# Layer 1 of a hybrid decoder step: queries, keys and values leave PSUM in one copy, and transposed keys leave their bank ahead of the queries

## The chip, the cores and the metric

The kernel runs on one core of a Trainium2 chip. The metric is the device time of one execution in microseconds (us). The engines are PE (TensorE), DVE (VectorE), ACT (ScalarE), POOL (GpSimd) and SP (SyncE, which issues the DMAs here).

## What is computed

The reference is one inference step of a two-layer decoder, for a prompt of 1024 tokens and 8 sample groups of 8 tokens (64 sample rows). Layer 0 is gated linear attention. Layer 1, which the change touches, is stick-breaking attention with 16 heads of 64:

```python
def sb_mixer(h, w_in, qn, kn, bias, w_out, k_past, v_past):
    ...
    u = h @ w_in
    q = rms_norm(u[..., :SB_W].reshape(bsz, length, SB_HEADS, SB_DH), qn)
    k = rms_norm(u[..., SB_W:2 * SB_W].reshape(bsz, length, SB_HEADS, SB_DH), kn)
    v = u[..., 2 * SB_W:3 * SB_W].reshape(bsz, length, SB_HEADS, SB_DH)
    g = u[..., 3 * SB_W:]
    ...
    o = sb_attend(q, k_all, v_all, bias, off).reshape(bsz, length, SB_W)
    return (o * jax.nn.silu(g)) @ w_out, k, v
```

In `sb_attend` the weight of key s for query t (s < t) is sigmoid(z[t, s]) times the product of (1 - sigmoid(z[t, j])) over the keys j between s and t. Normed keys and values are outputs too.

## The kernel before

Every fp32 operand of a large matmul is split into a high and a low half (`whi` and `wlo` for model weights, `qh` and `ql`, the halves of `kc`, the two `aT`), and products of halves are summed in PSUM. Layer 1 runs over 8 pairs of heads. For each pair, 9 tiles of rows (8 of 128 prompt rows, one of 64 sample rows) go through the input projection (`dense`, L293), and four times a gate's projection (`dense_t`, L315) stands between. Both sum in the two banks `acc`.

**Rows to queries and keys.** For each of the 9 tiles `qk_sums` squares queries and keys from the bank (ACT, L799), copies values (ACT, L801), sums the squares by head (DVE, L802) and takes the power -1/2 (POOL, L804). `qk_scale` multiplies queries and keys from the bank by it (DVE, L810) and makes the keys' output (POOL, L812). The bank is free after L810. The sample rows come out of `whole_rows` (L335, L336) in SBUF, as `xr`.

**Blocks.** Two tiles of rows at a time, 4 times a pair, `qk_p` transposes queries and keys on PE into one of the two banks `tr` (L829, four transposes). From there ACT copies the queries' high half four times (L853) and the keys' high half twice (L854, L855), and DVE makes the remainders: queries L856, L857, keys L858, L859. The text calls these the blocks 1 to 4 of a pair.

**Attention.** A unit is one head of the pair, 256 queries and 256 keys. `logits` multiplies (PE, L881, banks `z`) and ACT takes two sigmoids (`om` L884, `A` L885). `stick` scans on DVE (L904, L907) and multiplies (L912, L915). `turn` transposes the attention weights into a bank `tr` (PE, L928) and splits them (ACT L930, DVE L931). `weigh` multiplies by values (PE, L942, banks `o`). Behind a block's units `gate_b` adds two halves of the output (ACT L952, DVE L953, in turns) and multiplies by the gate (POOL, L954).

**What sets the order.** PE's order is written out: every step is put on one line of time by `at`, and PE follows it as it stands. Instructions of ACT, DVE, POOL and SP are put in order by the scheduler of the framework, by its own estimates. The scheduler also hands out the two buffers of each PSUM name; an instruction that writes a buffer waits for the last reader of what stood there. The next pair's model weights are split meanwhile (high halves ACT L219 or DVE L221, low halves POOL L222), most of it around block 4.

Of the kernel before, what the change touches and what calls it, by code (L numbers as in the profile page):

```python
# [9 lines left out]
F32 = mybir.dt.float32  # L10
# [3 lines left out]
AF = mybir.ActivationFunctionType  # L14
# [13 lines left out]
SH, DH = 16, 64  # L28
# [48 lines left out]
def tile_hybrid_decoder(ctx, tc, x_prompt, x_sample, state_gla, cache_k, cache_v, page_table,  # L77
# [3 lines left out]
    nc = tc.nc  # L81
# [46 lines left out]
    def sb(pool, name, shape, dtype=F32, bufs=2, tag=None):  # L128
        return pools[pool].tile(shape, dtype, name=name, tag=tag or name, bufs=bufs)
# [4 lines left out]
    def rows(t):  # L134
        return 128 if t < NP else NS
# [197 lines left out]
    def whole_rows(st, pool, n=512):  # L333
        up = sb(pool, "xr", [128, 512], F32, NX[pool])
        nc.scalar.activation(up[:64, :n], st["ps"][64:128, :n], AF.Copy)  # L335
        nc.vector.tensor_add(up[:64, :n], st["ps"][:64, :n], up[:64, :n])  # L336
        st["ps"] = up
# [78 lines left out]
    for t in range(NP + 1):  # L416
        st = {}
# [14 lines left out]
    for c, (c_0, n) in enumerate(CH):  # L432
        st = {}
# [228 lines left out]
    for h in range(GH):  # L662
# [3 lines left out]
        for c, (c_0, n) in enumerate(CH):  # L666
            st = {}
# [11 lines left out]
            for j, (key, out) in enumerate((("q", q_out), ("k", k_out))):  # L679
                lo, hi = a + (b - a) * 0.5 * j, a + (b - a) * 0.5 * (j + 1)  # L680
                dense_t(lo, hi, c_0, n, wqk,
                        lambda w, k, j=j: (w[k // 2], slice((k % 2) * 256 + j * 128, (k % 2) * 256 + j * 128 + 128)),
# [4 lines left out]
        for t in range(NP + 1):  # L687
            st = {}
# [50 lines left out]
    for c in range(2):  # L739
        w = weights([load_cols(w_out_a, D, k, c * 512, 0, 1, 512) for k in range(NK)])  # L740
        for t in range(NP + 1):
            st = {}
# [48 lines left out]
    def qk_sums(st, p, t):  # L791
        n = rows(t)
        if t == NP:
            whole_rows(st, "at1", 384)
        ps = st["ps"]
        sq = K1["sq"]
        q4 = ps[:n, :256].rearrange("p (h d) -> p h d", d=DH)
        ms = small.tile([128, 4], F32, name="ms4")
        nc.scalar.activation(sq[:n, :, :DH], q4, AF.Square, scale=1.0 / 8.0)  # L799
        st["v"] = sb("at1", "v", [128, 128])  # L800
        nc.scalar.activation(st["v"][:n], ps[:n, 256:384], AF.Copy)  # L801
        nc.vector.tensor_reduce(ms[:n], sq[:n], axis=AX.X, op=OP.add)  # L802
        st["rs"] = small.tile([128, 4], F32, name="rs4")
        nc.gpsimd.tensor_tensor(st["rs"][:n], ms[:n], half_exp[:n], op=OP.pow)  # L804

    def qk_scale(st, p, t):
        n, ps, rs = rows(t), st["ps"], st["rs"]
        q4 = ps[:n, :256].rearrange("p (h d) -> p h d", d=DH)
        qk = st["qk"] = sb("at1", "qk", [128, 4, DH], F32, 4)
        nc.vector.tensor_mul(qk[:n], q4, rs[:n, :, None].to_broadcast([n, 4, DH]))  # L810
        st["kout"] = sb("at1", "kout", [128, 2, DH])
        nc.gpsimd.tensor_mul(st["kout"][:n], qk[:n, 2:], K1["kn"][:n, None].to_broadcast([n, 2, DH]))  # L812

# [13 lines left out]
    def turn_qk(st, n, tr, slots):  # L827
        for j, x in enumerate(slots):
            nc.tensor.transpose(tr[:, x, :n], st["qk"][:n, 2 * j:2 * j + 2].rearrange("p a d -> p (a d)"), ident[:n, :n])  # L829
# [7 lines left out]
    def qk_p(sts, pair):  # L837

        tr = psum.tile([128, 4, 128], F32, name="tr")
        for x, st in enumerate(sts):
            turn_qk(st, 128, tr, (x, 2 + x))
        tr = tr.rearrange("p a s -> p (a s)")
        qp, kp, g = tr[:, :256], tr[:, 256:], K1["gains"]
        qh, kc = sb("at2", "qh", [128, 2, 256], F32R, NQ), sb("at2", "kc", [128, 2, 256], F32R, NKV)
        ql = K1["ql"][K1["turn"] % NQ]
        K1["turn"] += 1
        pair["q"].append((qh, ql))
        pair["k"].append(kc)  # L850
        up, dn = slice(0, 64), slice(64, 128)
        for dst, j, src in ((up, 0, up), (dn, 1, dn), (dn, 0, up), (up, 1, dn)):
            nc.scalar.activation(qh[dst, j], qp[src], AF.Copy, scale=g[src])  # L853
        nc.scalar.activation(kc[up, 0], kp[up], AF.Copy)  # L854
        nc.scalar.activation(kc[dn, 1], kp[dn], AF.Copy)  # L855
        nc.vector.scalar_tensor_tensor(ql[up, 0], qp[up], g[up], qh[up, 0], op0=OP.mult, op1=OP.subtract)  # L856
        nc.vector.scalar_tensor_tensor(ql[dn, 1], qp[dn], g[dn], qh[dn, 1], op0=OP.mult, op1=OP.subtract)  # L857
        nc.vector.tensor_sub(kc[dn, 0], kp[up], kc[up, 0])  # L858
        nc.vector.tensor_sub(kc[up, 1], kp[dn], kc[dn, 1])  # L859

    def gate_t(st, p, m, pair):
        ps, gt = st["ps"], sb("at1", "gt", [128, 256], F32, NG)
# [127 lines left out]
    for p in range(PAIRS):  # L990
# [4 lines left out]
        def columns(t, i, span):  # L995
            st = {}
            dense(i, t, w, st, span, 384)
            e = i + span
            at(e + 0.02, qk_sums, st, p, t)
            at(e + C_SC, qk_scale, st, p, t)  # L1000
            sts.append(st)
            if t < NP:
                at(max(e + C_SC, open2), v_parts, st, t, pair)
            if t == NP:
                at(e + C_TS, qk_s, st, p)
            elif t % 2 == 1:
                at(max(e + C_T, open2 + 0.01 * t), qk_p, sts[t - 1:], pair)
            at(max(e + C_T, open2) + 0.2, kv_store, st, p, t)
            return e
# [8 lines left out]
        for m in range(NP // 2):  # L1018
# [20 lines left out]
            if p == PAIRS - 1:  # L1039
                st = {}  # L1040
                for g in range(4):
                    n = 2 if g < 3 else 1
# [163 lines left out]
    for c, t in steps[:2 * NP - TAIL] + [(0, NP), (1, NP)] + steps[2 * NP - TAIL:]:  # L1206
        if t == NP and c == 0:
            i = max(i, s1 + S_GAP)
        st = {}
# [44 lines left out]
```

## Time and profile before

| | |
|---|---|
| Time, median of 3 runs | 1350.44 us (1347.35 to 1350.93) |
| The profiled execution | 1349.09 us, span 1347.4 us |
| PE busy over the span | 1269.9 us (94%) |
| DVE, ACT, POOL busy | 1011.1 (75%), 708.4 (53%), 515.5 (38%) us |
| TensorE clock granted | full in all 40 slices |
| DMA | 115.80 MB, mean 86 GB/s |

Busy times are sums over the instructions of an engine. A wait is the time an engine stood idle ahead of an instruction, put down to what was finished last among the things that it waited for. Layer 1's attention lies between about 535 and 1190 us of the span; a pair takes about 85 us there.

### The profile page before, as it was taken

To read this page: it belongs to the slowest core of one execution; us is meant where nothing else is said; L and a number is where in the kernel's file an instruction comes from. 1 tells how busy PE (TensorE), PEld (TensorE's weight loads), DVE (VectorE), ACT (ScalarE), POOL (GpSimd) and SP (SyncE) were. 2 spreads that over 40 slices of the span, in tenths; PEclk is the share of its full clock that TensorE was granted. 3 is DMA by queue.
4 is the path that set the end of the run, shared out by engine and by line. 5 is a ranking of instruction groups with operands and counts; after the bars stand their busy time and mean duration, and the time that the engine had idled before them with its cause. 6 is when DMAs were issued, how large, how long until landed. Compare 5 with 4: busy or idle time off the path is not lost.

```text
span 1347.4 us, 23358 instructions
## 1 busy us (share of the span) xinstructions
PE 1269.9 (94%) x8025; PEld 1128.5 (84%) x8025; DVE 1011.1 (75%) x2047; ACT 708.4 (53%) x1640; POOL 515.5 (38%) x847
## 2 busy tenths in 40 slices
PE   6899999999999999989989999899998999999998
PEld 5788888888887787889989899898898998978665
DVE  7857858759565357698898988988889889896543
ACT  6446245254352034566666766667667677763221
POOL 6222323223222215363453734646446464443000
PEclk9999999999999999999999999999999999999999
DMA  6311402403327443020120200202002022134862
GB/s 193 91 41 44 135 20 59 124 17 100 121 90 240 135 137 117 20 73 27 34 71 23 71 27 28 79 23 70 28 28 77 21 78 86 33 124 152 316 204 79
DMA packets 118456, 115.80 MB, mean 86 GB/s; under 512 B 11002, under 2 KB 97922, under 8 KB 118338
## 3 DMA queue, kind: packets, MB, share of 16 engines
q1 hardware_dynamic: 118338, 114.31, 27.5%
q8 instruction: 64, 1.05, 0.3%
q14 instruction: 54, 0.44, 0.1%
HBM read 83.61 MB, written 30.67 MB: 85 GB/s over the span
## 4 chain that ended last, share of the span: by engine, by line
PE 56%; DVE 25%; ACT 7%; issue 5%; POOL 4%; DMA 3%; SPq 0%; DVEq 0%; POOLq 0%; ACTq 0%
PE acc L293 33%; PE acc L315 6%; DVE run L907 4%; PE z L881 3%; PE tr L928 3%; PE o L942 2%; DVE aT L931 2%; DVE whi L221 2%; ACT qh L853 2%; DVE qk L810 1%; POOL rs L804 1%; DVE A L912 1%; DVE A L915 1%; PE o L544 1%; DVE run L904 1%
## 5 line engine op out<-in xcount | busy, mean ns | idle before, releaser
L293 PE MATMUL acc<-whi,h 128*128 128x512 f32 (+1 forms) x1728 | 538.1, 374 | 9.3 <-DVE qk L810 6.2
L293 PEld LDWEIGHTS acc<-whi,h 128*128 128x128 f32 x1728 | 312.8, 189 | 40.3 <-ACT sh L952 3.8
L293 PE MATMUL acc<-wlo,h 128*128 128x512 f32 (+1 forms) x864 | 322.6, 373 | 3.9 <-DVE wlo L222 2.5
L315 PE MATMUL acc<-h,whi 128*128 128x256 f32 (+5 forms) x832 | 191.7, 316 | 19.1 <-DVE qk L810 8.7
L222 POOL TENSOR_TENSOR wlo<-wr,whi 128x512 fp32r<-128x512 f32 x98 | 144.4, 1478 | 127.4 <-DVE whi L221 92.5
L293 PEld LDWEIGHTS acc<-wlo,h 128*128 128x128 f32 x864 | 162.5, 188 | 22.1 <-DVE wlo L222 3.2
L315 PEld LDWEIGHTS acc<-h,whi 128*128 128x128 f32 (+2 forms) x832 | 137.8, 185 | 26.2 <-issue 10.6
L907 DVE TENSOR_TENSOR_SCAN run<-om,run 128x256 f32<-128x256 f32 x192 | 141.8, 779 | 15.6 <-ACT om L884 15.1
L930 ACT ACTIVATE aT<-tr 128x512 fp32r<-128x512 f32 (+1 forms) x160 | 89.0, 556 | 82.8 <-PE tr L928 80.9
L884 ACT ACTIVATE om<-z,bias 128x512 f32<-128x512 f32 (+1 forms) x160 | 103.1, 644 | 48.3 <-PE z L881 39.6
L293 PE MATMUL acc<-w,h 128*128 128x384 f32 (+1 forms) x480 | 122.0, 365 | 0.8 <-DVE qk L810 0.8
L315 PE MATMUL acc<-h,wlo 128*128 128x256 f32 (+2 forms) x392 | 122.2, 312 | 0.3 <-POOL wlo L222 0.3
L931 DVE TENSOR_TENSOR aT<-tr,aT 128x512 fp32r<-128x512 f32 (+1 forms) x160 | 100.9, 631 | 9.7 <-ACT aT L930 7.4
L928 PE MATMUL tr<-ident,A 128*128 128x128 f32 x576 | 90.0, 274 | 18.6 <-DVE kc L859 8.4
L885 ACT ACTIVATE A<-z,bias 128x512 f32<-128x512 f32 (+1 forms) x160 | 102.4, 640 | 0.0
L942 PE MATMUL o<-aT,v 128*128 128x256 f32 (+1 forms) x640 | 98.1, 274 | 0.0
L928 PEld LDWEIGHTS tr<-ident,A 128*128 128x128 f32 x576 | 68.9, 140 | 34.0 <-ACT sq L799 9.0
L942 PEld LDWEIGHTS o<-aT,v 128*128 128x128 f32 x640 | 94.4, 188 | 1.7 <-DVE aT L931 1.0
L804 POOL TENSOR_TENSOR rs<-ms,half_exp 128x4 f32<-128x4 f32 (+1 forms) x72 | 86.2, 1198 | 21.3 <-DVE ms L802 18.8
L881 PE MATMUL z<-kc,qh 128*128 128x256 f32 x320 | 84.4, 286 | 7.2 <-DVE kc L858 7.2
L293 PEld LDWEIGHTS acc<-w,h 128*128 128x128 f32 x480 | 83.2, 189 | 6.3 <-issue 0.8
L899 POOL COPY run<-run 128x2 f32<-128x2 f32 x96 | 32.8, 342 | 135.7 <-DVE run L907 78.1
(273 smaller groups left out, 2488.7 us busy)
## 6 DMA issues: line engine op xcount, KB each, us to landing
wr<-in_w_in_b_dram SPq DMA_DIRECT2D x64, 256.0 KB, 3.0
wr<-in_w_in_a_dram SPq DMA_DIRECT2D x32, 256.0 KB, 2.9
kp<-in_cache_k_dram SPq DMA_DIRECT2D x16, 512.0 KB, 4.6
vp<-in_cache_v_dram SPq DMA_DIRECT2D x16, 512.0 KB, 4.9
o_d<-og SPq DMA_DIRECT2D x60, 128.0 KB, 1.8
x<-in_x_prompt_dram SPq DMA_DIRECT2D x8, 512.0 KB, 5.2
wr<-in_w_in_a_dram SPq DMA_DIRECT2D x32, 128.0 KB, 3.9
n<-in_state_gla_dram SPq DMA_DIRECT2D x8, 512.0 KB, 4.2
```

What stands on the lines that cost most here:

```text
L222: engine.tensor_sub(e.lo[:, :m], raw[:, :m], e.hi[:, :m])
L293: nc.tensor.matmul(st["ps"][:x.shape[1], :n], x, (w[k].hi if part == 0 else w[k].lo)[:, :n], start=first, stop=last)
L315: nc.tensor.matmul(st[key][:x.shape[1], :n], x, y, start=first, stop=last)
L804: nc.gpsimd.tensor_tensor(st["rs"][:n], ms[:n], half_exp[:n], op=OP.pow)
L881: nc.tensor.matmul(out, lhs, rhs, start=x == 0, stop=x == len(mm) - 1)
L884: nc.scalar.activation(u["om"][:, v0:], z[:, v0:], AF.Sigmoid, scale=-1.0, bias=K1["bias"][:, 1, hd:hd + 1])
L885: nc.scalar.activation(u["A"][:, v0:], z[:, v0:], AF.Sigmoid, bias=K1["bias"][:, 0, hd:hd + 1])
L907: nc.vector.tensor_tensor_scan(run[:, a, n - 1::-1], rev, rev, before[:, a, 0:1], op0=OP.mult, op1=OP.bypass)
L928: nc.tensor.transpose(tr[:, x], u["A"][:, col:col + 128], ident)
L930: nc.scalar.activation(hi[:, v0:], tr[:, v0:], AF.Copy)
L931: nc.vector.tensor_sub(lo[:, v0:], tr[:, v0:], hi[:, v0:])
L942: nc.tensor.matmul(q["po"][:, j, q0:], vs, part[:, x * 256 + q0:(x + 1) * 256], start=first and n == 0, stop=last and n == 3)
```

## The change

`qk_sums` makes one ACT copy of all 384 columns from the bank into a tile `qkv` in SBUF (four buffers); squares and products then read that tile, and the product is written in place. `qk_p` takes keys first, one engine after the other: ACT copies a high half, DVE takes its remainder, and so on for both halves of the keys and then of the queries. The two further query copies read the copies made before, in SBUF, and no longer the bank with a scale.

```diff
@@ qk_sums
-        q4 = ps[:n, :256].rearrange("p (h d) -> p h d", d=DH)
+
+        all3 = sb("at1", "qkv", [128, 384], F32, 4)
+        nc.scalar.activation(all3[:n], ps[:n, :384], AF.Copy)
+        st["qk"], st["v"] = all3[:, :256].rearrange("p (h d) -> p h d", d=DH), all3[:, 256:]
         ms = small.tile([128, 4], F32, name="ms4")
-        nc.scalar.activation(sq[:n, :, :DH], q4, AF.Square, scale=1.0 / 8.0)
-        st["v"] = sb("at1", "v", [128, 128])
-        nc.scalar.activation(st["v"][:n], ps[:n, 256:384], AF.Copy)
+        nc.scalar.activation(sq[:n, :, :DH], st["qk"][:n], AF.Square, scale=1.0 / 8.0)
@@ qk_scale
-        n, ps, rs = rows(t), st["ps"], st["rs"]
-        q4 = ps[:n, :256].rearrange("p (h d) -> p h d", d=DH)
-        qk = st["qk"] = sb("at1", "qk", [128, 4, DH], F32, 4)
-        nc.vector.tensor_mul(qk[:n], q4, rs[:n, :, None].to_broadcast([n, 4, DH]))
+        n, rs, qk = rows(t), st["rs"], st["qk"]
+        nc.vector.tensor_mul(qk[:n], qk[:n], rs[:n, :, None].to_broadcast([n, 4, DH]))
@@ qk_p
-        for dst, j, src in ((up, 0, up), (dn, 1, dn), (dn, 0, up), (up, 1, dn)):
-            nc.scalar.activation(qh[dst, j], qp[src], AF.Copy, scale=g[src])
         nc.scalar.activation(kc[up, 0], kp[up], AF.Copy)
+        nc.vector.tensor_sub(kc[dn, 0], kp[up], kc[up, 0])
         nc.scalar.activation(kc[dn, 1], kp[dn], AF.Copy)
+        nc.vector.tensor_sub(kc[up, 1], kp[dn], kc[dn, 1])
+        nc.scalar.activation(qh[up, 0], qp[up], AF.Copy, scale=g[up])
         nc.vector.scalar_tensor_tensor(ql[up, 0], qp[up], g[up], qh[up, 0], op0=OP.mult, op1=OP.subtract)
+        nc.scalar.activation(qh[dn, 1], qp[dn], AF.Copy, scale=g[dn])
         nc.vector.scalar_tensor_tensor(ql[dn, 1], qp[dn], g[dn], qh[dn, 1], op0=OP.mult, op1=OP.subtract)
-        nc.vector.tensor_sub(kc[dn, 0], kp[up], kc[up, 0])
-        nc.vector.tensor_sub(kc[up, 1], kp[dn], kc[dn, 1])
+
+        nc.scalar.activation(qh[dn, 0], qh[up, 0], AF.Copy)
+        nc.scalar.activation(qh[up, 1], qh[dn, 1], AF.Copy)
```

The new lines are L799 (copy), L802 (square), L803, L805, L809 (sums, power, product), L811 (keys' output), L851 to L854 (keys, ACT and DVE in turns), L855 to L858 (queries, likewise), L860 and L861 (copies in SBUF). Lines behind them stand 2 further down: the attention weights' copy L930 is now L932, their remainder L931 is L933, the scans L904 and L907 are L906 and L909. PE runs the same instructions in the same order; the order of the others is made anew.

DVE around block 4 of a pair, before. The scans are named SCALAR_TENSOR_TENSOR in the order and TENSOR_TENSOR_SCAN in the profile; `xr` are the sample rows.

```order
L912 TENSOR_TENSOR A<-A,run 128x256
L856 SCALAR_TENSOR_TENSOR ql_5790<-tr,gains,qh 64x256
L857 SCALAR_TENSOR_TENSOR ql_5790<-tr,gains,qh 64x256
L858 TENSOR_TENSOR kc<-tr,kc 64x256
L859 TENSOR_TENSOR kc<-tr,kc 64x256
L931 TENSOR_TENSOR aT_10136<-tr,aT_10135 128x512
L336 TENSOR_TENSOR xr<-acc,xr 64x384
L907 SCALAR_TENSOR_TENSOR run<-om,run 128x256 x2
L915 TENSOR_TENSOR A<-A,run 128x512
```

The same place with the change:

```order
L914 TENSOR_TENSOR A<-A,run 128x256
L852 TENSOR_TENSOR kc<-tr,kc 64x256
L854 TENSOR_TENSOR kc<-tr,kc 64x256
L933 TENSOR_TENSOR aT_10101<-tr,aT_10100 128x512
L336 TENSOR_TENSOR xr<-acc,xr 64x384
L856 SCALAR_TENSOR_TENSOR ql_5790<-tr,gains,qh 64x256
L909 SCALAR_TENSOR_TENSOR run<-om,run 128x256 x2
L917 TENSOR_TENSOR A<-A,run 128x512
L858 SCALAR_TENSOR_TENSOR ql_5790<-tr,gains,qh 64x256
L933 TENSOR_TENSOR aT_10160<-tr,aT_10159 128x384
```

The four operations of the block stood together; now attention weights, sample rows, two scans and a product stand between them.

ACT at the same place, with the change (before, L853 four times, L854 and L855 stood in one run, and `whi`, `aT`, `xr`, `om` and `A` followed):

```order
L851 ACTIVATE kc<-tr 64x256
L853 ACTIVATE kc<-tr 64x256
L932 ACTIVATE aT_10100<-tr 128x512
L219 ACTIVATE whi<-wr 128x512
L335 ACTIVATE xr<-acc 64x384
L855 ACTIVATE qh<-tr,gains 64x256
L886 ACTIVATE om<-z,bias 128x512
L887 ACTIVATE A<-z,bias 128x512
L219 ACTIVATE whi<-wr 128x512
L860 ACTIVATE qh<-qh 64x256
L799 ACTIVATE qkv<-xr 64x384
L219 ACTIVATE whi<-wr 128x512
```

L857, the second half of the queries, comes next; L853, L855 and L857 each wait for the DVE operation of the block ahead of them.

## Rows read from the trace of the kernel before

**Rows 1.** Windows: length; busy PE, PEld, DVE, ACT, POOL; PEclk; DMA share, GB/s.

```profile
535.00:1190.00 655.00, 610.82 (x4247) 582.97 (x4246) 564.53 (x1083) 445.70 (x952) 332.24 (x565) 1.00 0.17 49
784.00:869.20 85.20, 79.40 (x556) 75.77 (x555) 73.84 (x141) 57.41 (x122) 43.16 (x74) 1.00 0.16 45
840.00:860.00 20.00, 16.71 (x109) 15.09 (x107) 19.65 (x32) 14.89 (x32) 17.28 (x18) 1.00 0.35 100
```

**Rows 2.** Waits of PE, 530 to 1200: us in total, times, longest.

```profile
PE acc L315 <- DVE qk L810: 10.4, 7, 1.7
PE tr L928 <- DVE kc L859: 8.4, 6, 2.4
PE z L881 <- DVE kc L858: 7.2, 10, 1.4
PE acc L293 <- DVE qk L810: 7.0, 14, 1.2
PE tr L928 <- ACT sq L799: 4.5, 7, 1.0
```

**Rows 3.** Waits of DVE, the same stretch.

```profile
DVE ql L856 <- ACT kc L855: 34.2, 20, 4.8
```

**Rows 4.** Waits of ACT, the same stretch.

```profile
ACT sh L952 <- DVE og L953: 33.1, 20, 2.1
```

**Rows 5.** Instructions by form, 530 to 1200: busy us, mean ns.

```profile
L853 ACT ACTIVATE qh<-tr,gains 64x256 fp32r<-64x256 f32 x128 | 60.2, 470 | 21.6 <-PE tr L829 19.9
...
L930 ACT ACTIVATE aT<-tr 128x384 fp32r<-128x384 f32 x62 | 30.5, 491 | 43.7 <-PE tr L928 43.3
...
L799 ACT ACTIVATE sq<-acc 128x256 f32<-128x256 f32 x62 | 23.9, 385 | 11.6 <-DVE ms L802 6.6 <-PE acc L293 4.9
...
L801 ACT ACTIVATE v<-acc 128x128 f32<-128x128 f32 x62 | 17.6, 284 | 0.0
...
L859 DVE TENSOR_TENSOR kc<-tr,kc 64x256 fp32r<-64x256 f32 x32 | 13.6, 426 | 0.6
...
L855 ACT ACTIVATE kc<-tr 64x256 fp32r<-64x256 f32 x32 | 12.2, 380 | 0.6
...
L799 ACT ACTIVATE sq<-xr 64x256 f32<-64x256 f32 x8 | 3.3, 409 | 0.0
```

**Rows 6.** Line L810, whole span: ns min/median/max by form.

```profile
L810 DVE TENSOR_TENSOR qk<-acc,rs x64: 391/420/426, 527.6 to 1176.2; 128x256 f32<-128x256 f32 x64
...
L810 DVE TENSOR_TENSOR qk<-xr,rs x8: 406/1176/1514, 600.2 to 1194.8; 64x256 f32<-64x256 f32 x8
```

**Rows 7.** Timeline around block 4: start, us, instruction, idle before it.

```profile
845.36 0.47 DVE L856 SCALAR_TENSOR_TENSOR ql<-tr,gains,qh 64x256 fp32r<-64x256 f32 x1
...
846.11 0.69 ACT L884 ACTIVATE om<-z,bias 128x512 f32<-128x512 f32 x1
...
847.35 0.52 PE L928 MATMUL tr<-ident,A 128*128 128x128 f32 x3 [1.17 <-DVE kc L859]
...
849.82 1.51 DVE L915 TENSOR_TENSOR A<-A,run 128x512 f32<-128x512 f32 x1
...
851.38 0.66 PE L928 MATMUL tr<-ident,A 128*128 128x128 f32 x4
...
854.38 1.39 POOL L222 TENSOR_TENSOR wlo<-wr,whi 128x512 fp32r<-128x512 f32 x1
...
854.88 1.18 DVE L810 TENSOR_TENSOR qk<-xr,rs 64x256 f32<-64x256 f32 x1
```

**Rows 8.** Timeline at block 3 of the next pair.

```profile
909.31 0.69 DVE L915 TENSOR_TENSOR A<-A,run 128x512 f32<-128x512 f32 x1
...
910.75 0.38 ACT L855 ACTIVATE kc<-tr 64x256 fp32r<-64x256 f32 x1
...
911.17 0.48 DVE L856 SCALAR_TENSOR_TENSOR ql<-tr,gains,qh 64x256 fp32r<-64x256 f32 x1 [1.16 <-ACT kc L855]
...
912.73 0.35 PE L881 MATMUL z<-kc,qh 128*128 128x256 f32 x1 [0.54 <-DVE kc L858]
```

## What I expect of the change, and why

> **What bounds the kernel now.** The busy times by stretch come first [rows 1]. TensorE's granted clock is 1.00 throughout, so no clock is to be won back. In the 655.00 us of layer 1's attention part PE works 610.82, DVE 564.53, ACT 445.70, POOL 332.24. PE is the bound, and what the change can win on it is at most the 44 us in which PE idles. DVE stands close behind with 86%. The two further lines show where: one pair of heads lasts about 85 us, and in the 20 us from 840 to 860 DVE works 19.65. There the next pair's weights are split, DVE is the bound, and PE loses 3.3 us.
>
> The waits of PE say what ends its idle time [rows 2]. The two `acc` lines on the product L810 hold 10.4 + 7.0 = 17.4 us: a PSUM bank is not free before its rows have been squared, summed, raised to a power on POOL and multiplied. The `tr` and `z` lines belong to the blocks that turn queries and keys (`qk_p`). Waiting for L859 (8.4 us) is waiting for the bank of the block; for L858 (7.2 us) it is for finished keys. A transpose of weights needs nothing from the square L799: those 4.5 us are the same bank, whose last reader L859 ends just ahead of the square that the profile names. The waits of the other two engines show how such a block runs: DVE waits 34.2 us for ACT's last copy L855 before its first operation L856 [rows 3], and in `gate_b`, where the two engines take turns at one bank, ACT waits 33.1 us in 20 places for DVE [rows 4].
>
> **Part 1, the copy.** One ACT copy takes the place of the reading of PSUM by the square, the copy of values and the product. Its nearest row is a copy of the same form, 0.49 us (L930, 128x384); the values' copy of 0.28 us goes [rows 5]. That is 72 x 0.2 = 15 us more on ACT, which idles 209 us in the stretch: nothing on the path. The square reads SBUF now: for the sample rows, which were in SBUF already, it takes 0.41 instead of 0.39 us [rows 5], again nothing. PE's 17.4 us of waiting should go, since a copy that waits for the bank's matmuls alone ends about 0.5 us behind them and PE does not come back to the bank before the other one is filled: **-17.4**.
>
> The product is the price. From PSUM it took 0.39 to 0.43 us in all 64 places; from SBUF it took 1.18 us in the median of 8 [rows 6]; the one at 854.88 began beside POOL's L222, which reads SBUF, and ended 0.3 us behind it [rows 7]. All 72 read SBUF now. Lower bound nothing (0.41 us was also seen), upper bound 72 x 0.76 = 55 us of DVE time. What POOL does right behind the power decides: in the new order 49 of 72 times that is `kout`, which itself waits for the product, or a two-column copy; 23 times it is something longer. 23 x 0.76 = 17.5 us, and of a pair's nine products two fall into the stretch in which DVE is full, so that PE feels 2/9 of it: **+4**.
>
> The Trainium skill has this as a rule (SBUF — State Buffer, section "Who interferes with whom"): a VectorE instruction with two inputs in SBUF contends with a GpSimd instruction that reads SBUF, and the later one waits for the whole of the other; one with at most one input in SBUF does not. The trace agrees with both halves [rows 6]. Taken to its end, with every product behind a POOL operation, it makes the last rival below.
>
> **Part 2, the block.** Before, ACT ran six copies without a stop (4 x 0.47, 2 x 0.38) and DVE four operations behind them (two of about 0.43, two of about 0.47) [rows 5, 7]: 4.5 us to the release. Now ACT and DVE alternate: 0.38 + 0.43 + 0.38 + 0.43 + 4 x 0.47 = 3.5 us, and 7 handovers of 0.04 (L855 ends at 911.13, L856 begins at 911.17 [rows 8]): 3.8 us. Two copies of queries read SBUF; they have no scale, so I price them between L855's 0.38 and the old 0.47, on ACT beside other work: nothing. But that is an undisturbed chain. The orders of ACT and DVE show other work between its links, and each link waits for the other engine's queue. PE's order is unchanged, so the four blocks of a pair can be walked one by one.
>
> Block 1: the transposes that waited 7 times for the bank, 4.5 us, now get the other `tr` bank in the built kernel: **-4.5**. Block 2 had no stall and keeps slack. In the first pair the waits for keys (about 3 of the 7.2 us; seven third blocks hold the rest) should go, because ACT and DVE have little else to do there: **-3**.
>
> Block 3: DVE is free at 910.00 [rows 8]. From there, by when each ends: first subtraction 910.42, second key copy 910.84, second subtraction 911.3, ACT's copy of attention weights (0.49) 911.3, copy of q, k and v 911.8, first queries 912.3, their remainder 912.8, the square and the SBUF copy 913.05. PE had its keys at 912.73; it waits 0.3 longer, and up to 1.3 if it comes earlier by what it saved and DVE does not follow. I take 0.8 in each of 7 pairs: **+5.6**.
>
> Block 4 lies where DVE is full. DVE reaches the block at 845.36 [rows 7]. The second key copy waits for the subtraction that begins then; ACT, which ran through all its copies before, now ends the key copies at 846.2, the attention weights behind them at 846.8, a weight's high half and the sample rows at 847.9, the first queries at 848.4, and only then begins `om`, at 846.11 before. Behind it stand the second half of the queries and DVE's two scans and product (L907, L915), so the last reader of the bank, L858 in the new numbering, ends near 852.85. The first transposes after the block have the other bank, and wait for its reader as long as now for this one (1.17 us); the next ones, at 851.38 [rows 7], want the block's bank and wait about 1.4 us. With none of these delays the last reader ends at 850.3, and the old stall of 1.17 goes; with the longer form of L915 (1.51 us) it is some 0.8 later still. So -1.2 to +2.2 a pair, and I take +1.4 in 7 pairs, since ACT's order is certain: **+9.8**.
>
> One assumption in this walk is that a wait covers the whole bank. The trace shows it: L856 reads partitions 0 to 63 and still waits for L855, which reads 64 to 127 [rows 3].
>
> The Trainium skill would have it otherwise (PSUM — Partial Sum Buffer, section "PSUM bank collisions raise a hardware error"): two engines collide only on the same bank and the same 32 partitions, reads included, so the upper and lower halves need not wait for each other. By that, ACT would pass block 4 at its old time, its bank would be free by about 851, and blocks 3 and 4 would cost nothing: 5.6 + 9.8 = 15.4 us less than my sum, 1328. The waits in this program are by bank, so the sum goes by the row.
>
> **Sum**, against the profiled execution (1349.09 us, span 1347.4): 1349.1 - 17.4 + 4 - 4.5 - 3 + 5.6 + 9.8 = **1343.6**. That execution stands 1.35 us under the median of the runs, within their spread of 3.6. A difference under 0.3% (4 us) can't be told from none here.
>
> **Rivals.**
> *All waits go.* If the new order hides both blocks 3 and 4, PE gains the rest of its `tr` and `z` lines too: 17.4 + 8.4 + 7.2 + 4.5 = 37.5 us [rows 2], 1312. For it speaks that an undisturbed block is 0.7 us shorter and keys and first queries are ready 1.3 us sooner (2.7 against 4.0); against it that DVE is full around block 4 whatever the order is. A lesser form of it: if a wait covers only the half of the partitions that both engines read, both blocks cost nothing and the time is 1328; [rows 3] speaks against it, so 0.03. Chance 0.13 with that, anywhere from 1312 to 1335.
>
> *No change.* DVE is the bound wherever PE waits most: of the 3.3 us that PE loses from 840 to 860 [rows 1] nothing comes back if the same DVE work ends at the same time. If the longest stalls at the product (10.4 us) stay in this way, under another name, 1343.6 + 10.4 = 1354 is the far end, and half of it 1349. Chance 0.18.
>
> *The bank is held (slower).* Place: block 4, and the third block behind it. The taking of turns has a price in this program: ACT's wait in `gate_b` is 33.1 / 20 = 1.7 us a time [rows 4], and a block now has three such waits. If they delay the release not to 852.85 but two more turns, to 856, the transposes at 851.38 wait 4.7 us instead of 1.4, and `om` and the scans behind them move with it: 7 x 3.3 = 23, and 1343.6 + 23 = 1367. It decides as soon as blocks 3 and 4 cost more than the 17.4 + 4.5 + 3 - 4 = 20.9 us of the other terms, 3.0 us a pair; my sum has 2.2. Chance 0.18.
>
> *The product blocks DVE (slower).* If POOL is in the way of nearly all 72 products, DVE gains 55 us and works 95% of the stretch; with half of that on PE's path instead of 4 us, 1343.6 + 23 = 1367. Against it: after the power POOL mostly has nothing long to do. Chance 0.11.
>
> **Numbers.** My forecast, 1336 to 1346, has 0.40. Faster: 0.40 + 0.13 = 0.53; same 0.18; slower 0.18 + 0.11 = 0.29. The range leaves out the lower half of the first rival and the far end of the two slow ones, under 0.2 in all: 1318 to 1367.
>
> **What would show it.** Right: no PE wait for the product in the `acc` lines; no block-1 stall; in block 4 a wait of the weights' transposes for the last remainder of queries (L858) of 1 to 2 us a pair; ACT waits behind L853 for DVE; products of 0.42 us in some places and of over 1 us in others. Wrong: `acc` waits that stay because ACT's copy comes late; PE waits in blocks 3 and 4 above 3 us a pair or none; products that are all short or all long; DVE's busy time up by over 20 us.

## The result, and the profile after

The changed kernel takes 1360.92 us (median of 4 runs, 1358.62 to 1361.91) against 1349.93 us of the kernel before in the same comparison: a ratio of 1.0084, 95% interval 1.007 to 1.0097. It is slower by 11 us, where I had forecast that it would be faster by about 6. The profiled execution took 1361.91 us, with a span of 1360.1.

The waits of PE in the changed kernel, 530 to 1210 (us in total, times, longest), answer to [rows 2]:

```profile
PE tr L930 <- DVE aT L933: 19.6, 20, 2.5
PE z L883 <- ACT qh L860: 13.9, 10, 2.1
PE tr L828 <- DVE kTs L834: 5.3, 7, 1.3
PE tr L930 <- DVE ql L858: 5.2, 5, 1.0
PE tr L930 <- DVE A L914: 4.4, 6, 0.8
PE o L944 <- DVE aT L933: 4.2, 5, 0.9
```

No `acc` line is left: the 17.4 us of waiting for the product are gone, as the change promises. But the other lines have grown to over 50 us, and all of PE's waits together are more than before. PE now waits for a `tr` bank whose last reader is the remainder of the attention weights (L933), for the first queries in SBUF (L860), for the sample rows' keys (L834), for DVE's attention products (L914). All but L860 are DVE's.

ACT's longest line stands against [rows 4]; it is new:

```profile
ACT kc L853 <- DVE kc L852: 62.7, 32, 5.0
ACT sh L954 <- DVE og L955: 37.5, 19, 2.5
```

At the second key copy, L853, ACT stands 62.7 us, once in each of the 32 blocks, and behind it in ACT's queue stand copies that PE needs. ACT's wait in the turns of `gate_b` is little changed (37.5 us; before 33.1).

The windows of one pair, of the 20 us from its block 4 on, and of 5 us around a later wait answer to [rows 1] (length; busy PE, PEld, DVE, ACT, POOL; granted clock; DMA):

```profile
783.50:869.50 86.00, 78.76 (x555) 75.70 (x555) 75.17 (x141) 58.44 (x123) 44.06 (x75) 1.00 0.15 45
839.00:859.00 20.00, 16.03 (x106) 14.64 (x105) 16.81 (x25) 14.15 (x29) 13.38 (x15) 1.00 0.33 97
912.00:917.00 5.00, 4.66 (x22) 4.56 (x23) 3.66 (x9) 2.82 (x6) 1.81 (x4) 0.66 0.09 26
```

The pair lasts 86.0 instead of 85.2 us. Around block 4 DVE is no longer full: 16.81 us in 20, against 19.65, and PE has 16.03 against 16.71. Both engines now wait there. The last line shows the clock: behind a wait of PE of 1.77 us (912.34 below) the granted clock fell to the lower of its two levels, half of the upper, for some 3.4 us (a mean of 0.66 over 5 us). The trace holds five such falls. They are not what tells the two kernels apart: runs of the kernel before had them too (21 runs with a mean clock of 0.9969, against 0.9952 in 4 runs of the changed one), and among those 21 runs 0.001 of clock goes with 0.75 us, so the difference accounts for some 1.3 us of the 11. That price is a loose one (in 13 later runs of the same kernel 0.001 goes with 0.42 us).

Where the time goes within a pair is seen from the starts of the blocks' transposes on PE in the timelines (medians over pairs 2 to 7, us; "sample" is the transposes of the sample rows' queries and keys; the last five rows are experiments of the next section):

| kernel | block 1 to 2 | 2 to 3 | 3 to 4 | 4 to sample | sample to 1 | pair |
|---|---|---|---|---|---|---|
| before | 19.25 | 19.30 | 17.74 | 25.43 | 3.05 | 84.8 |
| changed | 18.51 | 18.23 | 18.90 | 26.45 | 3.95 | 86.0 |
| copy alone | 19.31 | 18.49 | 18.15 | 23.93 | 4.11 | 84.0 |
| block alone | 18.45 | 18.35 | 17.69 | 27.11 | 3.04 | 84.6 |
| no turns | 18.56 | 18.22 | 16.93 | 25.25 | 3.49 | 82.5 |
| no turns, bank copies | 19.31 | 18.48 | 17.91 | 23.87 | 4.11 | 83.7 |
| product on POOL | 18.48 | 18.22 | 17.91 | 26.07 | 3.04 | 83.7 |

The change wins 1.8 us in the first two stages and loses 3.1 in the last three. The third stage begins with block 3, which is seen in the timeline (start, us, instruction, idle before it):

```profile
908.75 0.69 DVE L917 TENSOR_TENSOR A<-A,run 128x512 f32<-128x512 f32 x1
...
909.47 0.42 DVE L852 TENSOR_TENSOR kc<-tr,kc 64x256 fp32r<-64x256 f32 x1
...
909.92 0.38 ACT L853 ACTIVATE kc<-tr 64x256 fp32r<-64x256 f32 x1 [2.02 <-DVE kc L852]
...
910.71 0.48 ACT L799 ACTIVATE qkv<-acc 128x384 f32<-128x384 f32 x1
...
911.08 0.46 ACT L855 ACTIVATE qh<-tr,gains 64x256 fp32r<-64x256 f32 x1
...
911.44 0.41 ACT L802 ACTIVATE sq<-qkv 128x256 f32<-128x256 f32 x1
...
911.87 0.41 ACT L860 ACTIVATE qh<-qh 64x256 fp32r<-64x256 f32 x1
...
912.34 0.39 PE L883 MATMUL z<-kc,qh 128*128 128x256 f32 x1 [1.77 <-ACT qh L860]
```

ACT had been done with the first key copy for 2.02 us when DVE, coming from a product (L917), made the first subtraction. Only then could ACT go on, and before the copy that PE waits for (L860) stood the second key copy, attention weights, the copy of q, k and v, the queries and a square.

Block 4, one pair earlier:

```profile
839.72 0.38 ACT L851 ACTIVATE kc<-tr 64x256 fp32r<-64x256 f32 x1 [0.36 <-PE tr L828]
...
841.04 2.81 DVE L906 TENSOR_TENSOR_SCAN run<-om,eye 128x128 f32<-128x128 f32 x2
...
844.41 0.42 DVE L852 TENSOR_TENSOR kc<-tr,kc 64x256 fp32r<-64x256 f32 x1
...
844.86 0.38 ACT L853 ACTIVATE kc<-tr 64x256 fp32r<-64x256 f32 x1 [4.76 <-DVE kc L852]
...
846.64 0.55 PE L930 MATMUL tr<-ident,A 128*128 128x128 f32 x3 [1.52 <-DVE aT L933]
...
847.29 0.67 ACT L886 ACTIVATE om<-z,bias 128x512 f32<-128x512 f32 x1
...
851.09 0.49 DVE L858 SCALAR_TENSOR_TENSOR ql<-tr,gains,qh 64x256 fp32r<-64x256 f32 x1 [0.88 <-ACT qh L857]
...
851.64 0.66 PE L930 MATMUL tr<-ident,A 128*128 128x128 f32 x4 [1.05 <-DVE ql L858]
```

ACT makes the first key copy at 839.72 and the second at 844.86, after standing for 4.76 us: DVE was at other work, the longest of it two scans (2.81 us, beside POOL's weights). PE then waits 1.52 us for the bank of the attention weights that ACT copied late, and 1.05 us for the last remainder of queries.

### The profile page after: what moved, and what is told of

Its sections match the earlier page's. It is cut to its first block, busy times and chain, and to the rows that moved or that the text cites. A ratio compares the mean times of both kernels' runs of the same rounds, so it can differ in the third digit from the quotient of the medians.

```text
span 1360.1 us, 23111 instructions
## 1 busy us (share of the span) xinstructions
PE 1273.4 (94%) x8025; PEld 1134.7 (83%) x8025; DVE 1020.9 (75%) x2047; ACT 717.4 (53%) x1640; POOL 518.3 (38%) x847
## 4 chain that ended last, share of the span: by engine, by line
PE 51%; DVE 26%; ACT 10%; issue 6%; POOL 5%; DMA 2%; SPq 0%; DVEq 0%; POOLq 0%; ACTq 0%
PE acc L293 31%; PE acc L315 6%; DVE run L909 4%; PE z L883 2%; DVE aT L933 2%; POOL rs L805 2%; DVE run L906 2%; DVE whi L221 2%; PE tr L930 2%; PE o L944 2%; DVE A L917 2%; DVE A L914 2%; ACT aT L932 2%; ACT om L886 1%; DVE qkv L809 1%
## 5 line engine op out<-in xcount | busy, mean ns | idle before, releaser
L293 PEld LDWEIGHTS acc<-whi,h 128*128 128x128 f32 x1728 | 316.1, 190 | 29.9 <-DVE xr L725 1.1
L222 POOL TENSOR_TENSOR wlo<-wr,whi 128x512 fp32r<-128x512 f32 x98 | 132.6, 1360 | 137.3 <-DVE whi L221 93.5
L909 DVE TENSOR_TENSOR_SCAN run<-om,run 128x256 f32<-128x256 f32 x192 | 143.4, 787 | 15.3 <-ACT om L886 13.1
L930 PE MATMUL tr<-ident,A 128*128 128x128 f32 x576 | 91.2, 277 | 29.3 <-DVE aT L933 19.6
L933 DVE TENSOR_TENSOR aT<-tr,aT 128x512 fp32r<-128x512 f32 (+1 forms) x160 | 101.0, 632 | 17.3 <-ACT aT L932 14.2
L932 ACT ACTIVATE aT<-tr 128x512 fp32r<-128x512 f32 (+1 forms) x160 | 88.5, 553 | 38.9 <-PE tr L930 36.1
L930 PEld LDWEIGHTS tr<-ident,A 128*128 128x128 f32 x576 | 69.9, 141 | 44.3 <-DVE aT L933 19.2
L883 PE MATMUL z<-kc,qh 128*128 128x256 f32 x320 | 85.3, 288 | 13.9 <-ACT qh L860 13.9
L906 DVE TENSOR_TENSOR_SCAN run<-om,eye 128x128 f32<-128x128 f32 (+1 forms) x128 | 89.5, 739 | 2.0 <-ACT om L886 1.3
L805 POOL TENSOR_TENSOR rs<-ms,half_exp 128x4 f32<-128x4 f32 (+1 forms) x72 | 79.4, 1103 | 26.1 <-DVE ms L803 22.9
L293 PEld LDWEIGHTS acc<-w,h 128*128 128x128 f32 x480 | 83.7, 190 | 5.1 <-issue 0.4
```

What stands on the lines that cost most here:

```text
L222: engine.tensor_sub(e.lo[:, :m], raw[:, :m], e.hi[:, :m])
L293: nc.tensor.matmul(st["ps"][:x.shape[1], :n], x, (w[k].hi if part == 0 else w[k].lo)[:, :n], start=first, stop=last)
L883: nc.tensor.matmul(out, lhs, rhs, start=x == 0, stop=x == len(mm) - 1)
L906: nc.vector.tensor_tensor_scan(run[:, a, n - 1::-1], rev, K1["eye"][:, 255:(255 - n) if n < 256 else None:-1], 0.0, op0=OP.mult, op1=OP.add)
L909: nc.vector.tensor_tensor_scan(run[:, a, n - 1::-1], rev, rev, before[:, a, 0:1], op0=OP.mult, op1=OP.bypass)
L930: nc.tensor.transpose(tr[:, x], u["A"][:, col:col + 128], ident)
```

## The experiments

**The two parts apart.** The first kernel has the new `qk_sums` and `qk_scale` with the old `qk_p`, the second the old ones with the new `qk_p`.

> The copy of queries, keys and values alone; the block is that of the kernel before. Theory A (the turns of ACT and DVE in the block cost the time): the PE waits for the product (17.4 us) go, the block's waits of the kernel before (about 20 us in the tr and z lines) stay, and the time is 1335 to 1345 us. Rival B (DVE is the bound around block 4, so that the same waits come back under another name): 1346 to 1354 us, with new PE waits for DVE's attention products and remainders behind block 4. Rival C (the copy itself costs, by ACT's added work): above 1354 us.

> The new order of the block alone (keys first, ACT and DVE in turns, two copies in SBUF); squares, sums and products are those of the kernel before. Theory A: the waits for the product stay (17 us) and those for keys in block 3 and for the bank in block 4 grow by about 1.2 and 1.4 us a pair, so 1360 to 1375 us. Rival B: the block costs little, 1347 to 1356 us. Rival C (the copy costs all of the loss): 1345 to 1352 us.

Copy alone: 1348.26 us, ratio 0.9986 (0.9976 to 0.9995). Block alone: 1350.45 us, 1.0002 (0.9992 to 1.0011). Neither part alone loses anything, so theory A falls for both. For the copy rival B holds: the waits for the product went and others came. The block alone lies in the ranges of rivals B and C. PE's waits in the copy alone:

```profile
PE tr L927 <- DVE kc L858: 11.2, 12, 1.8
PE z L880 <- DVE kc L857: 10.7, 10, 2.0
PE tr L828 <- DVE kTs L834: 6.6, 7, 1.3
PE tr L927 <- DVE A L914: 5.3, 6, 0.9
PE tr L927 <- DVE aT L930: 4.5, 9, 0.7
```

All of PE's waits from 530 to 1200 sum to 43.1 us before and to 43.4 in the copy alone. The wait for the block's bank stays (11.2 us; before 8.4 + 4.5 under two names [rows 2]), the wait for keys grew from 7.2 to 10.7, those for the sample rows' keys and for attention products are new. In the table the stage in which PE waited longest for the product (4 to sample) is 1.5 us shorter, and 1.1 of it is given back in the next one. What is left, 0.8 us in each of six pairs, goes in the last pair: from block 1 to the sample rows it takes 87.2 us in this trace, 82.2 before. There ACT and DVE also split the outputs for the final projection, and two falls of the clock lie in it. This trace is of the slowest of the 11 runs, 3.3 us above their median, so some of the loss may be this execution's alone; no other trace of this kernel was kept.

In the block alone the waits for the product fell too, from 17.4 to 11.7 us, without the copy:

```profile
PE acc L315 <- DVE qk L810: 6.1, 6, 1.0
PE acc L293 <- DVE qk L810: 5.6, 9, 1.4
```

**The turns.** Both kernels take ACT's four copies out of the bank first and DVE's four operations behind them, with keys first and the two further query copies in SBUF; the first on top of the new `qk_sums`, the second with the old one.

```diff
         nc.scalar.activation(kc[up, 0], kp[up], AF.Copy)
-        nc.vector.tensor_sub(kc[dn, 0], kp[up], kc[up, 0])
         nc.scalar.activation(kc[dn, 1], kp[dn], AF.Copy)
-        nc.vector.tensor_sub(kc[up, 1], kp[dn], kc[dn, 1])
         nc.scalar.activation(qh[up, 0], qp[up], AF.Copy, scale=g[up])
-        nc.vector.scalar_tensor_tensor(ql[up, 0], qp[up], g[up], qh[up, 0], op0=OP.mult, op1=OP.subtract)
         nc.scalar.activation(qh[dn, 1], qp[dn], AF.Copy, scale=g[dn])
+        nc.vector.tensor_sub(kc[dn, 0], kp[up], kc[up, 0])
+        nc.vector.tensor_sub(kc[up, 1], kp[dn], kc[dn, 1])
+        nc.vector.scalar_tensor_tensor(ql[up, 0], qp[up], g[up], qh[up, 0], op0=OP.mult, op1=OP.subtract)
         nc.vector.scalar_tensor_tensor(ql[dn, 1], qp[dn], g[dn], qh[dn, 1], op0=OP.mult, op1=OP.subtract)
```

> The changed kernel, with keys first and the two copies in SBUF, but in the block ACT makes its four copies out of the bank first and DVE its four operations behind them, so that the engines do not take turns. Theory A: block 3's wait for queries (1.7 us a pair) falls below 1 us, block 4's waits for the bank fall too, the product's waits stay away: 1335 to 1346 us. Rival B: the waits around block 4 stay, 1350 to 1358 us. Rival D (it is the clock: dips behind long PE waits cost some 7 us in the changed kernel): the time falls with the number of dips alone, so a run at a mean clock of 1.00 would be near 1353 us with the waits unchanged.

> The block of keys first, without turns and with two copies in SBUF, alone; squares and products are those of the kernel before. Theory A: block waits become a little shorter than before (four copies of the bank by ACT ahead of DVE, not six), the product's waits stay: 1343 to 1351 us. Rival B: 1347 to 1354 us, no change. If keys ahead of queries were itself the loss, it would be above 1356 us.

With the copy: 1334.28 us, 0.9878 (0.9863 to 0.9893). Without it: 1340.68 us, 0.9932 (0.9918 to 0.9945). So the same operations in another order are worth 26.6 us with the copy and 9.8 without it. Rival D falls: the clock of these four runs was 0.996, hardly above the changed kernel's. Block 3 without turns:

```profile
813.33 0.38 ACT L852 ACTIVATE kc<-tr 64x256 fp32r<-64x256 f32 x1
...
813.72 0.47 ACT L853 ACTIVATE qh<-tr,gains 64x256 fp32r<-64x256 f32 x1
...
814.21 0.47 ACT L854 ACTIVATE qh<-tr,gains 64x256 fp32r<-64x256 f32 x1
...
814.71 0.41 ACT L859 ACTIVATE qh<-qh 64x256 fp32r<-64x256 f32 x1
...
814.87 0.42 DVE L855 TENSOR_TENSOR kc<-tr,kc 64x256 fp32r<-64x256 f32 x1
...
816.19 0.19 PEld L883 LDWEIGHTS z<-kc,qh 128*128 128x128 f32 x1
```

ACT runs through its copies from 812.94 on, while DVE is still at its scans, and has copied the queries' high halves out of the bank before DVE begins (814.87). PE's logits hardly wait any more (0.8 us in 2 places for queries, against 13.9 in 10). In ACT's waits the second key copy is missing, and in the block alone, where the turns cost 9.8 us, it has half of the 62.7 us:

```profile
ACT kc L854 <- DVE kc L853: 30.7, 25, 4.4
...
ACT whi L219 <- DMA wr<-in_w_in_b_dram: 14.3, 6, 2.9
```

In part that is a change of name: in the block alone a model weight stands between the two key copies of block 4, and ACT waits 14.3 us for such weights' DMAs.

**Which turn.** The changed kernel with one half of the turns taken out: in the first run only the queries alternate, in the second only the keys.

```diff
 only the queries in turns
         nc.scalar.activation(kc[up, 0], kp[up], AF.Copy)
-        nc.vector.tensor_sub(kc[dn, 0], kp[up], kc[up, 0])
         nc.scalar.activation(kc[dn, 1], kp[dn], AF.Copy)
+        nc.vector.tensor_sub(kc[dn, 0], kp[up], kc[up, 0])
 only the keys in turns
         nc.scalar.activation(qh[up, 0], qp[up], AF.Copy, scale=g[up])
-        nc.vector.scalar_tensor_tensor(ql[up, 0], qp[up], g[up], qh[up, 0], op0=OP.mult, op1=OP.subtract)
         nc.scalar.activation(qh[dn, 1], qp[dn], AF.Copy, scale=g[dn])
+        nc.vector.scalar_tensor_tensor(ql[up, 0], qp[up], g[up], qh[up, 0], op0=OP.mult, op1=OP.subtract)
```

> The changed kernel with the keys out of turns (two ACT copies, then two DVE subtractions) and the queries still in turns. Turns together cost 26.6 us on top of the copy (1360.9 against 1334.3). Theory A1: the first handover costs, because ACT stands behind the first subtraction (62.7 us of ACT's waiting at the second key copy) while DVE is still at scans: then nearly all comes back, 1334 to 1342 us. Rival A2: the last handover costs, because the last remainder of queries holds the bank: then 1352 to 1361 us. Both: between.

> The changed kernel with the queries out of turns and the keys still in turns: the mirror of the run before. Theory A1: the loss stays, 1352 to 1361 us, with block 3's wait for queries above 1.2 us. Rival A2: most of it goes, 1334 to 1343 us.

Only the queries in turns: 1342.13 us, 0.9943 (0.9924 to 0.9961), at the upper edge of A1's range. Only the keys: 1359.56 us, 1.008 (1.0059 to 1.0101), the changed kernel's time. The first handover is what costs most, as A1 says; the queries' turns cost 0.65%, some 9 us, beside the kernel without turns, and nothing more once the keys have made ACT wait. A2 falls: with the keys in turns, the bank's last reader came 2.6 us sooner in block 4 (9.3 instead of 11.9 us behind the transposes' end, means of pairs 2 to 7) and the time stayed; with the queries in turns it came later than that (10.2 us) in a much faster kernel, and in the block alone latest of all (14.8 us) in a kernel no slower than the one before. ACT's longest wait in either, with the wait at the first query copy in the first:

```profile
ACT sh L954 <- DVE og L955: 41.1, 20, 3.8
...
ACT qh L855 <- DVE kc L854: 30.2, 23, 2.1
```

```profile
ACT kc L853 <- DVE kc L852: 62.5, 32, 5.1
```

**DVE's load.** Two relieve DVE in the changed kernel: the sample rows' two scaled copies go to ACT, or the product, which here reads the copy in SBUF, goes to POOL.

```diff
-        nc.vector.tensor_scalar(K1["qTs"][:, p], tr[:, 0, :NS], K1["qn"], None, op0=OP.mult)
+        nc.scalar.activation(K1["qTs"][:, p], tr[:, 0, :NS], AF.Copy, scale=K1["qn"])
...
-        nc.vector.tensor_mul(qk[:n], qk[:n], rs[:n, :, None].to_broadcast([n, 4, DH]))
+        nc.gpsimd.tensor_mul(qk[:n], qk[:n], rs[:n, :, None].to_broadcast([n, 4, DH]))
```

> The changed kernel with the sample rows' two scaled copies (qTs, kTs) on ACT in place of DVE. They end a wait of PE of 5.3 us in 7 places (0.75 a pair). If that wait stands for itself, the time falls by about 5 us, to 1355 to 1357 us. If DVE's lateness as a whole is behind it (it does not follow PE, which comes earlier), the wait moves on to the block behind: 1359 to 1362 us.

> The changed kernel with the product of queries and keys by the power on POOL in place of DVE, which only the copy to SBUF allows. It takes 36.9 us of work and 15.7 us of waiting for POOL off DVE and puts some 72 times 0.8 to 1 us on POOL (half idle). If DVE's load is what PE waits for in the changed kernel: below 1352 us. If the turns are what costs, whatever DVE has to do: 1356 to 1362 us. If the product on POOL itself comes too late for the transposes: above 1362 us.

The sample rows on ACT: 1357.58 us, 1.0065 (1.0045 to 1.0086). That is 0.2% under the changed kernel, less than the 5 us of the wait, and the two intervals overlap: whether it gains anything here isn't shown. PE still waits 2.5 us for those keys, now from ACT. The product on POOL: 1343.87 us, 0.9971 (0.9953 to 0.9989), by the ratios 1.1% or 15 us under the changed kernel. POOL takes 0.73 us for it:

```profile
L809 POOL TENSOR_TENSOR qkv<-qkv,rs 128x256 f32<-128x256 f32 x63 | 45.7, 726 | 3.9
```

So DVE's load is part of the loss, as the expectation of a time below 1352 us had it. ACT's wait at the second key copy only falls from 62.7 to 55.3 us, so the turns still cost (the same kernel without them, in the last section, has 0.9875), and the run doesn't say how much of the 15 us comes through a shorter turn.

**Holding the bank.** The changed kernel, with the copy made as before, but the product reading the bank.

```diff
+        q4 = st["ps"][:n, :256].rearrange("p (h d) -> p h d", d=DH)
-        nc.vector.tensor_mul(qk[:n], qk[:n], rs[:n, :, None].to_broadcast([n, 4, DH]))
+        nc.vector.tensor_mul(qk[:n], q4, rs[:n, :, None].to_broadcast([n, 4, DH]))
```

> The changed kernel, with the copy, but the product reads queries and keys from the bank again, so that the bank is held until the product as before. Theory E (the early release itself makes the turns dear: PE runs ahead of DVE to the block, and ACT stands behind the first subtraction for DVE's backlog): waits for the product come back (about 12 us), ACT's wait at the second key copy falls from 62.7 towards 31 us, as in the block alone, and the time is 1348 to 1354 us in spite of the waits. Rival F (ACT's added copy is what costs): 1358 to 1365 us.

1384.52 us, 1.027 (1.0253 to 1.0287). Theory E was right on ACT's wait and wrong on the time:

```profile
ACT kc L854 <- DVE kc L853: 28.8, 23, 3.0
```

```profile
PE acc L293 <- DVE qkv L810: 18.2, 12, 3.0
PE acc L315 <- DVE qkv L810: 18.0, 7, 3.7
```

ACT's wait fell to the half, but the product now waits for a copy, a square, a sum and a power, and PE for the product: more than twice the 17.4 us of the kernel before. So this run can't price the early release; whether the turns would be cheap with the bank held at its old length stays open. What it does show is where the longer wait comes from. In block 1 of a pair, in the changed kernel and in the block alone:

```profile
783.47 0.66 PE L828 MATMUL tr<-ident,qkv 128*128 128x128 f32 x4 [0.75 <-DVE kTs L834]
...
784.16 0.38 ACT L851 ACTIVATE kc<-tr 64x256 fp32r<-64x256 f32 x1 [0.46 <-PE tr L828]
...
786.16 0.42 DVE L852 TENSOR_TENSOR kc<-tr,kc 64x256 fp32r<-64x256 f32 x1
```

```profile
781.88 0.60 PE L829 MATMUL tr<-ident,qk 128*128 128x128 f32 x4
...
782.52 0.38 ACT L852 ACTIVATE kc<-tr 64x256 fp32r<-64x256 f32 x1 [1.31 <-PE tr L829]
...
782.93 0.42 DVE L853 TENSOR_TENSOR kc<-tr,kc 64x256 fp32r<-64x256 f32 x1
```

In the changed kernel DVE's first subtraction begins 2.1, 0.9 and 2.6 us behind the transposes' end in blocks 1 to 3, in the block alone 0.45, 0.45 and 1.65, and in this run, with the bank held again, 0.46, 0.45 and 1.59 (means of pairs 2 to 7). This run has the copy and ACT's added work too, so it is the early release that brings PE's transposes before DVE is ready for the block.

**The copies in SBUF.** The kernel without turns, with the two further query copies read from the bank with a scale, as before.

```diff
-        nc.scalar.activation(qh[dn, 0], qh[up, 0], AF.Copy)
-        nc.scalar.activation(qh[up, 1], qh[dn, 1], AF.Copy)
+        nc.scalar.activation(qh[dn, 0], qp[up], AF.Copy, scale=g[up])
+        nc.scalar.activation(qh[up, 1], qp[dn], AF.Copy, scale=g[dn])
```

> The kernel without turns, with the two further copies of queries taken from the bank with a scale, as before, not from SBUF. If the SBUF source matters, by two copies of 0.47 us less between the transposes and the first subtraction, the time rises by up to 0.9 us a block, 1338 to 1348 us; if DVE is busy in that time anyway, 1333 to 1337 us.

1345.38 us, 0.9978 (0.9964 to 0.9991): 1.0% or some 13 us above the kernel without turns by the ratios, and stage by stage the copy alone (table). Keys ahead of queries thus bring nothing by themselves. The copies in SBUF do: less by their length (0.42 instead of 0.47 us) than because DVE no longer waits for them. Without turns, in block 1, its first operation begins 2.0 us behind the transposes and its last ends at 3.9; with the copies from the bank it is 2.8 and 4.6 (means of pairs 2 to 7).

**Where the copy's gain goes.** The copy alone, with the product on POOL.

> The copy alone (block of the kernel before), with the product on POOL. The copy alone ended all 17.4 us of waits for the product and moved the time by 2 us only. If DVE's backlog behind block 4 is what took their place (waits for the sample rows' keys, for attention products and remainders), the product off DVE lets the gain through: 1334 to 1342 us. If it is the block's own six copies, which this run leaves as they are: 1344 to 1350 us.

1346.35 us, 0.9981 (0.9972 to 0.9991): this can't be told from the copy alone. So it is not the product on DVE that keeps the gain of the copy back; the block's lines move little:

```profile
PE tr L927 <- DVE kc L858: 10.3, 11, 2.0
PE z L880 <- DVE kc L857: 8.8, 10, 2.0
```

In this trace the last pair takes 90.7 us, with three falls of the clock, though pairs 2 to 7 take 83.0; it too is of the slowest of its runs. With the kernels of the last section this answers in part where the gain went: with six copies out of the bank ahead of DVE the copy of q, k and v gains 2 us, where PE waited 17.4 us for the product; with four it gains 6.4 us (1334.28 against 1340.68 us), where PE waited 9.6. Where the rest goes is not shown.

**A version that beats both.** No turns with the product on POOL, and the same with the sample rows' copies on ACT too.

> The kernel without turns, with the product on POOL. On the changed kernel the product on POOL brought 1.1%, the missing turns bring 2.0%. If both work on the same thing (DVE's lateness), the sum is less than theirs: 1325 to 1334 us. If they add up: 1316 to 1322 us. If POOL comes too late: above 1336 us.

> No turns, the product on POOL and the sample rows' two copies on ACT. The last gave 0.2% on the changed kernel, by a wait that is only 2.7 us in all without turns: 0 to 3 us under the run before this one, whatever that gives.

1331.16 us, 0.9875 (0.9859 to 0.9892), and 1329.01 us, 0.9853 (0.9837 to 0.987). Without turns the product on POOL adds nothing that can be told from none beside 0.9878. So the gains don't add up, which the expectation reads as one cause for both, DVE's lateness; the time lies in the range that it gave for that, 1325 to 1334 us. The sample rows on ACT give 2 us, inside the expected 0 to 3. The windows of the last one:

```profile
535.00:1190.00 655.00, 624.64 (x4375) 601.34 (x4374) 590.54 (x1036) 472.51 (x991) 396.11 (x648) 1.00 0.18 53
```

PE works 624.64 of 655.00 us; before it was 610.82 [rows 1].

## Why the prediction was wrong

**The copy, -17.4: the step that failed.** I had PE's waits for the product go, and they did, all of them. I then took them as time won. The copy alone, which removes the same waits, is faster by 2 us, and PE's waits as a whole stay (43.1 and 43.4 us). The prediction named what would prevent it, under *No change*: DVE work that ends at the same time, so that stalls stay under another name. That rival got 0.18; by the runs it belonged in the sum. In one pair, the 1.72 + 0.60 us of waits behind block 4 before were replaced in the copy alone by 0.93 (attention product) and 0.92 us (sample rows' keys), and in the changed kernel by 0.86 (attention weights), 0.80 (attention product) and 0.75 us (sample rows' keys).

**The product, +4.** It cost next to nothing: 64 products of full size took at most 0.5 us, and those that wait for POOL are sample rows', as before: 6 over 1 us, where I had counted with 23. Line L809 over the whole span:

```profile
L809 DVE TENSOR_TENSOR qkv<-qkv,rs x72: 390/422/1509, 527.9 to 1207.9; 128x256 f32<-128x256 f32 x64, 64x256 f32<-64x256 f32 x8
```

The Trainium skill's rule on the shared port (SBUF — State Buffer, "Who interferes with whom") is not contradicted: its case is rare here. How rare depends on the order of the two engines: in the copy alone, with the same product, 6 of full size took 1.3 us too. The rival in which the product blocks DVE falls.

**The block, -4.5 - 3 + 5.6 + 9.8.** As waits of the changed kernel these terms were near. From block 1 to 2 the pair is 0.74 us shorter (forecast 0.6). The first pair, from its first block to the next pair's, takes 74.7 instead of 79.3 us (forecast 3 less). Block 3's wait rose from 0.56 to 1.73 us: 1.2 a pair, forecast 0.8 with 1.3 as its end. In block 4 the last reader of the bank ended 11.9 us behind the transposes, the 12 us of the walk; the three waits there (0.54, 1.52, 1.05) are 1.6 us more than before (0.37, 1.17), forecast 1.4. But as time they were not, and that is the second step that failed: they sum to +7.9, and the block alone costs nothing; and for the turns, the 5.6 + 9.8 = 15.4 us of these two blocks, the runs show 9.8 us without the copy and 26.6 with it. I took the two parts of the change to add up, and they do not. Nor did I see which turn matters most: I put the price on the bank and its last reader, the queries' remainder. The runs put it on the first: with the keys out of turns 19 us come back, with the queries out of turns half a us.

**The slower rival** had the sign and the place, not the mechanism: it had the bank held until the queries' last remainder, and the run with only the keys in turns refutes that. Its condition, that blocks 3 and 4 cost over 3.0 us a pair more, was not met (2.7); the sum turned because the other side of the balance, 20.9 us, shrank.

**The signs.** All that I had named for being right came: no wait for the product, none in block 1, 1.05 us for the last remainder of queries, ACT's waits behind L853, products of both lengths. One that I had named for being wrong came too, PE waits above 3 us a pair in blocks 3 and 4 (4.8, before 2.1). The first group told of the waits that I had walked through, not of the time.

**The waits by bank.** L853 reads partitions 64 to 127 and still waited in all 32 blocks for L852, which reads 0 to 63. These two also write one tile, `kc`; but with only the queries in turns L855, which writes `qh` and reads 0 to 63, waited 30.2 us in 23 places for L854, which writes `kc` and reads 64 to 127. That agrees with [rows 3]; by the Trainium skill's rule of bank and quadrant (PSUM — Partial Sum Buffer, "PSUM bank collisions raise a hardware error") the wait would not be needed, and no kernel here was built without it.

**What stays open:** the price in time of the two parts together, 11 us where each alone costs nothing. By the table the changed pair is 2.2 us longer than the sum of what the parts do to it, about 0.7 us in block 2's stage and 0.8 in each of the two behind. Shown is that the turns of the keys carry the loss, and that with the copy DVE comes later to blocks 1 to 3 than in the block alone, so that ACT stands longer at the second key copy (62.7 us; in the block alone 30.7, and some of the 14.3 us for weights that stand between the two key copies there). Part of the copy's gain was also no longer there to be had beside the new block, which had brought the waits for the product to 11.7 us by itself. That these two make up the 11 us is argued, not shown: the run that should have priced the early release (holding the bank) took a cost of its own.

## What to carry to other kernels

Where two engines with queues in order read one PSUM bank, and a wait covers the whole bank as here, let the first make all its copies and the second follow: in turns, the first one stands through the backlog of the second, with everything queued behind it. Don't add up the gains of two changes that meet at one busy engine; run each alone and both together. A wait that ends at a busy engine is not yet time won when it is removed; look for what that engine finishes next, and ask whether it would be ready sooner. Of copies that read the same values twice, the second can read the first's result and leave the bank to the other engine.

## What the runs showed of the hardware

The two copies of queries with source and result in SBUF and no scale took 0.42 us, against 0.38 for copies of the same size out of PSUM without a scale [rows 5] and 0.47 with one. A POOL product of 128x256 in SBUF took 0.73 us beside DVE's 0.42. TensorE's granted clock fell to the lower of its two levels for some 3.4 us behind some of PE's waits of 1.7 us and more and not behind others of the same length (behind 1.77 us at 912.34, but not behind 1.73 us in the pair before, nor behind 2.4 us in the kernel before [rows 2], whose trace has no fall in this stretch).
